# Two low-part subtractions per gate/up block handed from VectorE to accumulating transfers

## The chip, the cores and the metric

The kernel runs on one core of a Trainium2 chip. The metric is the device time of one execution in microseconds; the median of three runs of the kernel before is 1597.2 us (1596.22 to 1598.54).

## What is computed

One layer of a hybrid decoder block on 256 tokens of width 2048, in float32: an input projection, sliding-window attention beside a state-space mixer, two branch projections and a merged output projection, then the gated feed-forward part that the change touches, then a gated extra embedding and a last norm. The part that matters here:

```python
f = rmsnorm(h, g_ffn[i])
h = h + (jax.nn.silu(f @ w_gate[i]) * (f @ w_up[i])) @ w_down[i]
```

`w_gate` and `w_up` are 2048 x 5632, `w_down` is 5632 x 2048.

## The kernel before

Every float32 product is made of three matmuls in the fp32r type: weights and activations are each split into a high part (rounded to fp32r) and a low part (what rounding left), and high x high, high x low and low x high are summed in PSUM. So each weight chunk is loaded, cast to fp32r by ScalarE (the high part, tile `wh`), and subtracted by VectorE (the low part, tile `wl` = `wr` - `wh`).

Gate and up are computed by `wide_block` (L268), called by `hidden` (L987) once for each of the 11 column blocks of 512. A block takes the contraction dimension of 2048 in eight pairs of 128-row slices, `kp` = 0 to 7. For each pair there are two chunks, one of `w_gate` (`q` = 0) and one of `w_up` (`q` = 1), each 128 partitions x 1024 elements (512 KB).

- Pairs 0, 1, 3, 5 and 7 are plain: per chunk one load into `wr` (L293-294), the cast into `wh` (L296), the subtraction into `wl` (L298), and twelve matmuls of 512 columns (L248), so 24 matmuls per pair.
- Pairs 2, 4 and 6 use a seven-product scheme: VectorE first makes four sums of weight slices in `tr` (L316), then the two raw chunks and `tr` are split (L324, L325) into `wh`/`wl` and `th`/`tl`; 21 matmuls per pair.

So a block has 183 matmuls of 512 columns, and eight small transposes of the block before it run in its first pair.

Nothing in the source orders the engines against each other: the framework's scheduler sets the order of each engine's instructions, and the pools set how far ahead they may run. The pools that count here: `wraw` with 4 buffers (`wr`), `whi` with 4 (`wh`), `wlo` with 3 (`wl`), and `big` with 17 buffers of 8 KB per partition, which `tr`, `th`, `tl`, `mid` share with the activations that live through the stage. Weight loads are all issued by SP; in gate and up POOL has nothing to do.

The 11 blocks come in three thirds (4, 4 and 3 blocks); after each third, `nblock` (L178) multiplies its result with `w_down`.

Of the kernel before, what the change touches and what calls it, by code (L numbers as in the profile page):

```python
# [11 lines left out]
F32 = mybir.dt.float32  # L12
F32R = mybir.dt.float32r
I32 = mybir.dt.int32
AF = mybir.ActivationFunctionType
ALU = mybir.AluOpType
AX = mybir.AxisListType

P = 128
# [4 lines left out]
NB = 512  # L24
# [37 lines left out]
def block_kernel(ctx: ExitStack, tc: tile.TileContext, x, x_t, p_t, positions, vecs, rows, g_final,  # L62
                 w_in, w_attn_br, w_ssd_br, w_o, w_gate, w_up, w_down, w_ple_gate,
                 w_ple_proj, out):
    nc = tc.nc
# [3 lines left out]
    wraw_p = ctx.enter_context(tc.tile_pool(name="wraw", bufs=4))  # L69
    whi_p = ctx.enter_context(tc.tile_pool(name="whi", bufs=4))  # L70
    wlo_p = ctx.enter_context(tc.tile_pool(name="wlo", bufs=3))
# [5 lines left out]
    def big(shape, dtype=F32, name="big"):  # L77
        return big_p.tile(shape, dtype, name=name, tag="big")
# [186 lines left out]
        nc.vector.tensor_tensor(out=dst[:, :, 1], in0=fm, in1=dst[:, :, 0].bitcast(F32),  # L265
                                op=ALU.subtract)

    def wide_block(halves, lhs, nk, forms, pumps=1):  # L268

# [11 lines left out]
        def load(q, kp, dst):  # L283
            w, col0 = halves[q]
            nc.sync.dma_start(out=dst, in_=w[2 * kp * P:2 * (kp + 1) * P, col0:col0 + NB].rearrange(
                "(k p) n -> p k n", p=P))

        for kp in range(np_):
            ev, od = lhs(2 * kp), lhs(2 * kp + 1)
            tok = [[[x[:, t * P:(t + 1) * P] for x in k] for k in (ev, od)] for t in range(NT)]  # L290
            if kp not in forms:
                for q in range(2):
                    wr = wraw_p.tile([P, 2, NB], F32, name="wr", tag="wr")  # L293
                    load(q, kp, wr)
                    wh = whi_p.tile([P, 2, NB], F32R, name="wh", tag="wh")
                    nc.scalar.copy(out=wh, in_=wr)  # L296
                    wl = wlo_p.tile([P, 2, NB], F32R, name="wl", tag="wl")
                    nc.vector.tensor_tensor(out=wl, in0=wr, in1=wh.bitcast(F32), op=ALU.subtract)  # L298
                    for k in range(2):
                        for t in range(NT):  # L300
                            sums[2 * t + q].add(tok[t][k], (wh[:, k], wl[:, k]))
                    pump(pumps)
                continue
# [259 lines left out]
    for t in range(NT):  # L563
        nc.vector.scalar_tensor_tensor(out=dtv[:, t], in0=accs[1][t][:, W2 - SSM_H:W2],
                                       scalar=r1[:, t:t + 1],
                                       in1=row[:, R_DTB:R_DTB + SSM_H],
# [203 lines left out]
    for t in range(NT):  # L770
# [3 lines left out]
                             scale=r1[:, t:t + 1])  # L774
# [144 lines left out]
    for j in range(4):  # L919
        accs = nblock(w_in, GAO + j * NB, lhs_u, KD)  # L920
        for t in range(NT):
            nc.scalar.activation(out=merged[t][:, cols(j)], in_=accs[0][t], func=AF.Sigmoid,
                                 scale=r1[:, t:t + 1])
    drain(heads)
    r2 = const.tile([P, NT], F32, name="r2")
    for j in range(4):
        accs = nblock(w_attn_br, j * NB, lambda k: stat(attnT, k), 8)
        for t in range(NT):
            nc.vector.tensor_tensor(out=merged[t][:, cols(j)], in0=accs[0][t],
                                    in1=merged[t][:, cols(j)], op=ALU.mult)  # L930
# [14 lines left out]
    for j in range(4):  # L945
        accs = nblock(w_in, GSO + j * NB, lhs_u, KD)
        gs = [roll("gs") for _ in range(NT)]
        for t in range(NT):
            nc.scalar.activation(out=gs[t], in_=accs[0][t], func=AF.Sigmoid,
                                 scale=r1[:, t:t + 1])  # L950
# [35 lines left out]

    def hidden(j, dst):  # L987
        sums, parts = wide_block(((w_gate, j * NB), (w_up, j * NB)), lambda k: stat(hT, k), KD,
                                 hforms)
        act = [roll("act") for _ in range(NT)]  # L990
        for i, (o, op) in enumerate(((act[0], ALU.add), (parts[1], ALU.subtract),
                                     (act[1], ALU.add), (parts[3], ALU.subtract))):
            nc.vector.tensor_tensor(out=o, in0=sums[i], in1=parts[i], op=op)
        for t in range(NT):
            nc.scalar.activation(out=act[t], in_=act[t], func=AF.Silu, scale=r3[:, t:t + 1])
            nc.vector.scalar_tensor_tensor(out=act[t], in0=parts[2 * t + 1],
                                           scalar=r3[:, t:t + 1], in1=act[t], op0=ALU.mult,
                                           op1=ALU.mult)
        for i in range(2):
            side.append(lambda i=i: transpose_pair(act, i * 2 * P, dst, 2 * i))  # L1000
# [180 lines left out]
```

## Time and profile before

| | before |
|---|---|
| median of 3 runs | 1597.2 us (1596.22 to 1598.54) |
| the profiled execution's own time | 1597.2 us |
| its span in the trace | 1595.5 us |
| TensorE busy / VectorE busy / ScalarE busy | 99% / 69% / 51% |
| TensorE share of the chain that ended last | 95% |
| mean granted TensorE clock | 0.998 |
| bytes moved by DMA | 296.63 MB, mean 186 GB/s |

The busy share says who works all the time; the chain of waits says what the end of the kernel hung on. Matmuls are shown with their latency (0.39 us for 512 columns), and one starts before the last has ended, so that TensorE reads as busy even where it loses time between two starts. Lost time has to be looked for in the distance between starts, in the chain, and in the waits of the weight loads.

### The profile page before, as it was taken

The page shows a single profiled execution, that of the slowest core. Times are in us where ns is not written, and L with a number is a line of the kernel's source. Part 1 is how long each engine was busy: PE and PEld are TensorE (multiplying, and loading weights), DVE is VectorE, ACT ScalarE, POOL GpSimd, SP SyncE. Part 2 cuts the span into 40 slices and gives each one's busy share as a digit, 9 for nine tenths or more (in the row PEclk, how much of TensorE's full clock was granted, in tenths as well). Part 3 has the DMA queues.
Part 4 walks back from the last instruction along what each step waited for, and adds up shares of the span by engine and source line. Part 5 has one row for each costly group of instructions (what it writes and reads, how often), then busy time and mean ns, then how long its engine had stood idle before and what let it go on. Part 6 is the DMA issues. An engine that isn't in the chain of part 4 may idle for free.

```text
span 1595.5 us, 19878 instructions
## 1 busy us (share of the span) xinstructions
PE 1580.3 (99%) x7315; PEld 1304.8 (82%) x7315; DVE 1101.7 (69%) x1334; ACT 821.5 (51%) x1034; POOL 130.8 (8%) x136
## 2 busy tenths in 40 slices
PE   9999999999999999999999999999999999999997
PEld 7988888888888888888888888888888888887886
DVE  7776766666655555456788975598886578876673
ACT  6654665555643444445565553455554345546552
POOL 1014224143210000000000000000000000000000
PEclk9999999999999999999999999999999999999999
DMA  8666435555656666655566666666666666666661
GB/s 268 178 195 184 138 105 158 158 160 158 179 184 219 191 190 185 197 184 184 185 199 186 197 198 195 188 208 188 198 198 190 193 197 205 189 224 221 202 207 53
DMA packets 152564, 296.63 MB, mean 186 GB/s; under 512 B 9539, under 2 KB 9667, under 8 KB 152083
## 3 DMA queue, kind: packets, MB, share of 16 engines
q1 hardware_dynamic: 151168, 290.76, 58.9%
q0 software_dynamic: 576, 3.47, 0.7%
q8 instruction: 57, 0.93, 0.2%
q10 hardware_dynamic: 720, 1.14, 0.2%
q14 instruction: 43, 0.33, 0.1%
HBM read 293.23 MB, written 2.10 MB: 185 GB/s over the span
## 4 chain that ended last, share of the span: by engine, by line
PE 95%; DMA 1%; ACT 1%; DVE 1%; issue 1%; POOL 0%; POOLq 0%; DVEq 0%; ACTq 0%; SPq 0%
PE acc L204 17%; PE acc L206 17%; PE acc L205 17%; PE aux L248 15%; PE acc L248 14%; PE aux L205 2%; PE aux L204 2%; PE aux L206 2%; PE aux L150 1%; DMA wr<-in_w_down_dram 1%; PE aux L709 1%; DVE wl L195 1%; PE aux L886 1%; PE acc L233 1%; PE acc L234 0%
## 5 line engine op out<-in xcount | busy, mean ns | idle before, releaser
L195 DVE TENSOR_TENSOR wl<-wr,wh 128x1024 fp32r<-128x1024 f32 (+1 forms) x356 | 452.2, 1275 | 323.0 <-PE acc L205 251.8
L193 ACT CAST wh<-wr 128x1024 fp32r<-128x1024 f32 (+1 forms) x356 | 367.7, 1035 | 433.6 <-PE acc L206 343.4
L204 PE MATMUL acc<-wh,uT 128*128 128x512 f32 (+1 forms) x640 | 250.7, 392 | 0.6 <-ACT cb L438 0.6
L206 PE MATMUL acc<-wh,uT 128*128 128x512 f32 (+1 forms) x640 | 243.9, 381 | 0.0
L205 PE MATMUL acc<-wl,uT 128*128 128x512 f32 (+1 forms) x640 | 243.5, 381 | 0.0
L296 ACT CAST wh<-wr 128x1024 fp32r<-128x1024 f32 x110 | 115.7, 1053 | 144.9 <-PE acc L248 62.3
L248 PE MATMUL aux<-wh,hT 128*128 128x512 f32 x546 | 179.2, 391 | 0.0
L298 DVE TENSOR_TENSOR wl<-wr,wh 128x1024 fp32r<-128x1024 f32 x110 | 133.2, 1222 | 43.3 <-issue 33.8
L248 PE MATMUL acc<-wh,hT 128*128 128x512 f32 x466 | 155.0, 393 | 0.0
L204 PEld LDWEIGHTS acc<-wh,uT 128*128 128x128 f32 x640 | 120.3, 188 | 22.9 <-issue 1.4
L206 PEld LDWEIGHTS acc<-wh,uT 128*128 128x128 f32 x640 | 120.2, 188 | 23.0
L205 PEld LDWEIGHTS acc<-wl,uT 128*128 128x128 f32 x640 | 120.4, 188 | 22.4 <-issue 1.0
L248 PEld LDWEIGHTS aux<-wh,hT 128*128 128x128 f32 x546 | 102.3, 188 | 21.4
L248 PE MATMUL aux<-wl,hT 128*128 128x512 f32 x273 | 106.3, 390 | 0.0
L248 PEld LDWEIGHTS acc<-wh,hT 128*128 128x128 f32 x466 | 87.3, 188 | 18.1
L205 PE MATMUL acc<-wl,actT 128*128 128x512 f32 x256 | 99.8, 390 | 0.0
L206 PE MATMUL acc<-wh,actT 128*128 128x512 f32 x256 | 99.8, 390 | 0.0
L204 PE MATMUL acc<-wh,actT 128*128 128x512 f32 x256 | 99.6, 389 | 0.0
L248 PE MATMUL acc<-wl,hT 128*128 128x512 f32 x233 | 90.7, 389 | 0.0
L324 ACT CAST wh<-wr 128x1024 fp32r<-128x1024 f32 x66 | 55.2, 838 | 55.4 <-PE aux L248 18.1
L325 DVE TENSOR_TENSOR tl<-tr,th 128x2048 fp32r<-128x2048 f32 x33 | 75.5, 2288 | 6.4 <-ACT th L324 6.4
L324 ACT CAST th<-tr 128x2048 fp32r<-128x2048 f32 x33 | 63.0, 1910 | 14.9 <-DVE tr L316 13.0
(344 smaller groups left out, 2719.8 us busy)
## 6 DMA issues: line engine op xcount, KB each, us to landing
wr<-in_w_in_dram SPq DMA_DIRECT2D x144, 512.0 KB, 3.6
wr<-in_w_gate_dram SPq DMA_DIRECT2D x88, 512.0 KB, 3.8
wr<-in_w_up_dram SPq DMA_DIRECT2D x88, 512.0 KB, 4.4
wr<-in_w_down_dram SPq DMA_DIRECT2D x88, 512.0 KB, 4.5
wr<-in_w_ssd_br_dram SPq DMA_DIRECT2D x32, 512.0 KB, 3.9
wr<-in_w_o_dram SPq DMA_DIRECT2D x32, 512.0 KB, 4.4
wr<-in_w_ple_gate_dram SPq DMA_DIRECT2D x32, 512.0 KB, 4.4
wr<-in_w_in_dram SPq DMA_DIRECT2D x32, 256.0 KB, 4.1
```

What stands on the lines that cost most here:

```text
L150: nc.tensor.transpose(out=ps[:, j, t * P:(t + 1) * P], in_=src[t][:, c:c + P], identity=ident)
L193: nc.scalar.copy(out=wh, in_=wr)
L195: nc.vector.tensor_tensor(out=wl, in0=wr, in1=wh.bitcast(F32), op=ALU.subtract)
L204: nc.tensor.matmul(o, hi[:, ts], wh[:, kk, cs], start=(k == 0), stop=False)
L205: nc.tensor.matmul(o, hi[:, ts], wl[:, kk, cs], start=False, stop=False)
L206: nc.tensor.matmul(o, lo[:, ts], wh[:, kk, cs], start=False, stop=(k == nk - 1))
L233: nc.tensor.matmul(o, hi[:, ts], wh[:, i], start=(k == 0), stop=False)
L248: nc.tensor.matmul(self.tile, a, b, start=self.first, stop=self.left == 0)
L296: nc.scalar.copy(out=wh, in_=wr)
L298: nc.vector.tensor_tensor(out=wl, in0=wr, in1=wh.bitcast(F32), op=ALU.subtract)
L324: nc.scalar.copy(out=xh, in_=x)
L325: nc.vector.tensor_tensor(out=xl, in0=x, in1=xh.bitcast(F32), op=ALU.subtract)
```

## The change

In each block the low part of two plain `w_up` chunks, those of pairs 3 and 7, is no longer made by VectorE. `prepare` loads the chunk, ScalarE casts it into one half of a tile of the `big` pool (`both`), and writes the negative of the same rounded value into the other half (an activation with scale -1); then a DMA issued by POOL reads the chunk once more from HBM and adds it onto that half in SBUF. `early={0: 3, 4: 7}` says where it stands in the program: pair 3's chunk is prepared ahead of pair 0, pair 7's ahead of pair 4.

```diff
+        def prepare(q, kp):
+            w, col0 = halves[q]
+            wr = wraw_p.tile([P, 2, NB], F32, name="wr", tag="wr")
+            load(q, kp, wr)
+            both = big([P, 2, 2, NB], F32R, name="both")
+            wh, wl = both[:, 0], both[:, 1]
+            nc.scalar.copy(out=wh, in_=wr)
+            nc.scalar.activation(out=wl, in_=wr, func=AF.Copy, scale=-1.0)
+            nc.gpsimd.dma_start(out=wl, in_=w[2 * kp * P:2 * (kp + 1) * P, col0:col0 + NB].rearrange(
+                "(k p) n -> p k n", p=P), accum_op=ALU.add)
+            ready[q, kp] = wh, wl
+
+        ready = {}
         for kp in range(np_):
+            if kp in early:
+                prepare(1, early[kp])
...
                 for q in range(2):
-                    wr = wraw_p.tile([P, 2, NB], F32, name="wr", tag="wr")
-                    load(q, kp, wr)
-                    wh = whi_p.tile([P, 2, NB], F32R, name="wh", tag="wh")
-                    nc.scalar.copy(out=wh, in_=wr)
-                    wl = wlo_p.tile([P, 2, NB], F32R, name="wl", tag="wl")
-                    nc.vector.tensor_tensor(out=wl, in0=wr, in1=wh.bitcast(F32), op=ALU.subtract)
+                    if (q, kp) in ready:
+                        wh, wl = ready[q, kp]
+                    else:
...
-                                 hforms)
+                                 hforms, early={0: 3, 4: 7})
```

The scheduler orders the engines anew. Three places of the third block show it; the numbers behind the names are those of single tiles.

VectorE around pair 4, before. `wl_7157` and `wl_7175` are the low parts of pair 3 (gate, up), `wl_7199` and `wl_7201` those of pair 4's raw chunks, `wl_7235` and `wl_7253` those of pair 5, `tl_7203` the low part of pair 4's sums:

```order
L298 TENSOR_TENSOR wl_7157<-wr_7153,wh_7155 128x1024
L325 TENSOR_TENSOR tl_7125<-tr_7115,th_7124 128x2048
L298 TENSOR_TENSOR wl_7175<-wr_7171,wh_7173 128x1024
L316 TENSOR_TENSOR tr_7193<-wr_7189,wr_7190 128x512
L316 TENSOR_TENSOR tr_7193<-wr_7190 128x512
L325 TENSOR_TENSOR wl_7199<-wr_7189,wh_7198 128x1024
L316 TENSOR_TENSOR tr_7193<-tr_7193,wr_7189 128x512
L325 TENSOR_TENSOR wl_7201<-wr_7190,wh_7200 128x512
L316 TENSOR_TENSOR tr_7193<-tr_7193,wr_7189 128x512
L298 TENSOR_TENSOR wl_7235<-wr_7231,wh_7233 128x1024
L325 TENSOR_TENSOR tl_7203<-tr_7193,th_7202 128x2048
L298 TENSOR_TENSOR wl_7253<-wr_7249,wh_7251 128x1024
```

The same place with the change (`wl_7129` is the low part of pair 2's up chunk, `wl_7163` pair 3 gate, `wl_7205` and `wl_7207` pair 4, `wl_7241` pair 5 gate, `tl_7209` pair 4's sums):

```order
L346 TENSOR_TENSOR wl_7129<-wr_7118,wh_7128 128x512
L346 TENSOR_TENSOR tl_7131<-tr_7121,th_7130 128x2048
L318 TENSOR_TENSOR wl_7163<-wr_7159,wh_7161 128x1024
L337 TENSOR_TENSOR tr_7199<-wr_7195,wr_7196 128x512
L337 TENSOR_TENSOR tr_7199<-wr_7196 128x512
L346 TENSOR_TENSOR wl_7205<-wr_7195,wh_7204 128x1024
L337 TENSOR_TENSOR tr_7199<-tr_7199,wr_7195 128x512
L346 TENSOR_TENSOR wl_7207<-wr_7196,wh_7206 128x512
L337 TENSOR_TENSOR tr_7199<-tr_7199,wr_7195 128x512
L318 TENSOR_TENSOR wl_7241<-wr_7237,wh_7239 128x1024
L346 TENSOR_TENSOR tl_7209<-tr_7199,th_7208 128x2048
```

Pair 3's up chunk is gone from the list. With three `wlo` buffers a `wl` is written where the third `wl` before it stood: `wl_7235` takes the buffer of `wl_7175` (pair 3 up), `wl_7241` that of `wl_7163` (pair 3 gate).

TensorE at pair 4's products with the sums, before; `wh_7233` and `wl_7235` belong to pair 5:

```order
L248 MATMUL acc_7109<-th_7202,hforms_5620 128x512
L248 MATMUL acc_7110<-th_7202,hforms_5620 128x512
L248 MATMUL acc_7108<-th_7202,hforms_5620 128x512
L248 MATMUL aux_7019<-th_7202,hT_5618 128x512
L248 MATMUL aux_7017<-wh_7233,hT_5618 128x512
L248 MATMUL aux_7017<-wl_7235,hT_5618 128x512
L248 MATMUL acc_7109<-tl_7203,hforms_5620 128x512
L248 MATMUL acc_7109<-th_7202,hforms_5620 128x512
L248 MATMUL acc_7110<-tl_7203,hforms_5620 128x512
L248 MATMUL acc_7110<-th_7202,hforms_5620 128x512
```

and with the change:

```order
L248 MATMUL acc_7115<-th_7208,hforms_5620 128x512
L248 MATMUL acc_7115<-tl_7209,hforms_5620 128x512
L248 MATMUL acc_7115<-th_7208,hforms_5620 128x512
L248 MATMUL acc_7116<-th_7208,hforms_5620 128x512
L248 MATMUL acc_7116<-tl_7209,hforms_5620 128x512
L248 MATMUL acc_7116<-th_7208,hforms_5620 128x512
```

The count of matmuls is the same; the scheduler no longer moves products with `th` and two of pair 5 ahead of the first product with `tl`, which comes at the pair's eleventh matmul instead of its sixteenth.

ScalarE from pair 2's sums to pair 4's, before:

```order
L296 CAST wh_7155<-wr_7153 128x1024
L324 CAST th_7124<-tr_7115 128x2048
L296 CAST wh_7173<-wr_7171 128x1024
L324 CAST wh_7198<-wr_7189 128x1024
L324 CAST wh_7200<-wr_7190 128x512
L296 CAST wh_7233<-wr_7231 128x1024
L324 CAST th_7202<-tr_7193 128x2048
```

and with the change, where `both_7191` is pair 7's up chunk:

```order
L345 CAST th_7130<-tr_7121 128x2048
L316 CAST wh_7161<-wr_7159 128x1024
L296 CAST both_7191<-wr_7189 128x1024
L297 ACTIVATE both_7191<-wr_7189 128x1024
L345 CAST wh_7204<-wr_7195 128x1024
L345 CAST wh_7206<-wr_7196 128x512
L316 CAST wh_7239<-wr_7237 128x1024
L345 CAST th_7208<-tr_7199 128x2048
```

The accumulating DMA that POOL issues for `both_7191` waits for the second of its two rows. On SP the load of pair 7's up chunk takes the place in the queue that pair 3's had, and pair 3's stands ahead of pair 0's.

## Rows read from the trace of the kernel before

**Rows 1.** The page's busy times: engine, busy us, share of the span, instructions.

```profile
PE 1580.3 (99%) x7315; PEld 1304.8 (82%) x7315; DVE 1101.7 (69%) x1334; ACT 821.5 (51%) x1034; POOL 130.8 (8%) x136
```

**Rows 2.** The chain, two pairs of the third block: start us, us, what, count.

```profile
865.98 0.68 PE acc L248 x3
...
869.38 1.61 PE acc L248 x6
870.99 5.44 PE aux L248 x24
876.43 0.68 PE acc L248 x3
```

**Rows 3.** The chain, the same two pairs in the fifth block.

```profile
1039.37 0.68 PE acc L248 x3
...
1041.41 2.04 PE acc L248 x9
1043.45 6.12 PE aux L248 x27
1049.57 0.68 PE acc L248 x3
```

**Rows 4.** Waits from 700 to 1450 us: waiter <- releaser: us, times, longest.

```profile
PEld aux L248 <- DVE tl L325: 5.6, 15, 0.4
...
PEld acc L248 <- DVE tl L325: 4.2, 12, 0.4
```

**Rows 5.** Timeline of weight loads: start us, us, what [idle before <- releaser].

```profile
869.33 0.19 PEld L248 LDWEIGHTS acc<-tl,hforms 128*128 128x128 f32 x1 [0.37 <-DVE tl L325]
```

**Rows 6.** Timeline of VectorE in the third block.

```profile
859.38 1.28 DVE L316 TENSOR_TENSOR tr<-wr 128x512 f32<-128x512 f32 x2
...
864.17 0.69 DVE L325 TENSOR_TENSOR wl<-wr,wh 128x512 fp32r<-128x512 f32 x1
865.85 1.23 DVE L298 TENSOR_TENSOR wl<-wr,wh 128x1024 fp32r<-128x1024 f32 x1 [0.99 <-issue]
866.99 2.29 DVE L325 TENSOR_TENSOR tl<-tr,th 128x2048 fp32r<-128x2048 f32 x1
```

**Rows 7.** Timeline of ScalarE in the third block.

```profile
863.34 1.05 ACT L296 CAST wh<-wr 128x1024 fp32r<-128x1024 f32 x1 [2.15 <-PE aux L248]
864.30 1.90 ACT L324 CAST th<-tr 128x2048 fp32r<-128x2048 f32 x1
```

**Rows 8.** Timeline of TensorE around the first product with tl.

```profile
868.99 0.39 PE L248 MATMUL aux<-wl,hT 128*128 128x512 f32 x1
869.33 0.50 PE L248 MATMUL acc<-tl,hforms 128*128 128x512 f32 x1
869.67 0.39 PE L248 MATMUL acc<-th,hforms 128*128 128x512 f32 x1
```

**Rows 9.** Windows, one whole block: us, busy us (count) per engine, clock, DMA share, GB/s.

```profile
860.49:903.69 43.20, 43.20 (x192) 34.86 (x192) 38.36 (x44) 23.48 (x25) 0.00 (x0) 1.00 0.64 194
```

**Rows 10.** DMA issues: tile, queue, count, KB each, median us to landing.

```profile
wr<-in_w_up_dram SPq DMA_DIRECT2D x88, 512.0 KB, 4.4
...
gfin<-in_g_final_dram POOLq DMA_DIRECT2D x1, 1024.0 KB, 4.6
```

**Rows 11.** The page's DMA queues: packets, MB, share of 16 engines.

```profile
q1 hardware_dynamic: 151168, 290.76, 58.9%
```

**Rows 12.** The tile wr, 820 to 945 us: how long its loads took.

```profile
DMA to landing us min/median/max: 3.5/3.8/5.1
```

**Rows 13.** Timeline of POOL from 500 to 1460 us.

```profile
1335.77 0.59 POOL L1040 DMA_DIRECT2D pt<-in_p_t_dram  x1 [559.50 <-PE aux L150]
1398.29 0.53 POOL L1043 DMA_DIRECT2D gfin<-in_g_final_dram  x1 [61.93 <-DVE tl L325]
```

**Rows 14.** Timeline of ScalarE at the end of the first block's preparations.

```profile
774.94 0.61 ACT L264 CAST hforms<-fm 128x512 fp32r<-128x512 f32 x1
```

**Rows 15.** The chain in the first block: pair 2, and pair 4.

```profile
779.70 0.68 PE acc L248 x3
...
790.09 0.68 PE acc L248 x3
```

More of the change, by code (lines that the diff above doesn't have):

```diff
@@ L266, in token_forms, with wide_block @@
                                 op=ALU.subtract)
-    def wide_block(halves, lhs, nk, forms, pumps=1):
+    def wide_block(halves, lhs, nk, forms, pumps=1, early={}):
         psum.reverse()
@@ L292, in wide_block @@
                 for q in range(2):
-                    wr = wraw_p.tile([P, 2, NB], F32, name="wr", tag="wr")
-                    load(q, kp, wr)
-                    wh = whi_p.tile([P, 2, NB], F32R, name="wh", tag="wh")
-                    nc.scalar.copy(out=wh, in_=wr)
-                    wl = wlo_p.tile([P, 2, NB], F32R, name="wl", tag="wl")
-                    nc.vector.tensor_tensor(out=wl, in0=wr, in1=wh.bitcast(F32), op=ALU.subtract)
+                    if (q, kp) in ready:
+                        wh, wl = ready[q, kp]
+                    else:
+                        wr = wraw_p.tile([P, 2, NB], F32, name="wr", tag="wr")
+                        load(q, kp, wr)
+                        wh = whi_p.tile([P, 2, NB], F32R, name="wh", tag="wh")
+                        nc.scalar.copy(out=wh, in_=wr)
+                        wl = wlo_p.tile([P, 2, NB], F32R, name="wl", tag="wl")
+                        nc.vector.tensor_tensor(out=wl, in0=wr, in1=wh.bitcast(F32),
+                                                op=ALU.subtract)
                     for k in range(2):
```

## The prediction

> **What bounds the kernel now.** The page's busy times come first: TensorE is busy for 1580.3 of 1595.5 us, VectorE for 69% and ScalarE for 51% of the span [rows 1]. Removing VectorE work is therefore worth only what TensorE waits for it. A matmul's row lasts 0.39 us, but 24 of them take 5.44 us in the chain [rows 2, 8], so one starts every 0.227 us; time is lost where two starts stand further apart. In the chain I set two equal pieces of work side by side: pair 2 with pair 3 (21 + 24 matmuls) runs from 865.98 to 876.43 us in the third block, 10.45 us [rows 2], and from 1039.37 to 1049.57 us in the fifth, 10.20 us [rows 3], which is just 45 x 0.227. So 0.25 us is lost in the third block's pair.
>
> The timeline shows where. Between the matmul at 868.99 and the first with `tl` at 869.33 lie 0.34 us, and again 0.34 us to the next [rows 8]: twice 0.11 too much, as the weight load waited for `tl` [rows 5] and the load behind it could not be made ahead. `tl` takes VectorE 2.29 us and begins at 866.99, behind a `wl` of 1.23 us that itself began only at 865.85 after an idle 0.99 us [rows 6]. That `wl` is the next plain pair's gate chunk; it waited for a `wlo` buffer, the one of the last plain pair's up chunk, which TensorE finishes just before the seven-product pair starts. So the delay is not VectorE's load but its order: `tl` stands in line behind an instruction that waits for TensorE. The waits count 15 + 12 of these, 9.8 us of idle weight loads [rows 4]. By the order of the two engines 25 of the 33 seven-product pairs have this `wl` ahead of their `tl`; at 0.37 us each [rows 5] these are 9.25 of the 9.8 us, and two in the first block are smaller.
>
> **The change part by part.**
>
> *Removed: 22 subtractions of 1.22 us on VectorE* (1.23 in [rows 6]), two per block. A block has 38.36 us of VectorE work in 43.20 us [rows 9]; it becomes some 35.9. In itself this is worth nothing, as VectorE is not the bound.
>
> *Moved: what waits ahead of `tl`.* With the up chunk of pair 3 out of the `wlo` buffers, the `wl` ahead of pair 4's `tl` takes the buffer of pair 3's gate chunk, which is free twelve matmuls (2.7 us) earlier. Pair 7's up chunk does the same for the next block's start. By the order of the changed program only 2 `tl` still stand behind a `wl` that waits for the very end of the pair before: pair 6 of the first block and pair 2 of the second. In return TensorE wants `tl` five matmuls (1.1 us) earlier. That order is the one of the fifth block, where no time is lost [rows 3]. The term is 25 - 2 = 23 pairs x 0.25 = **5.75 us gained**; its ends are 0 (each wait replaced by another) and 27 x 0.25 = 6.75.
>
> *Is a new last wait close behind?* The tightest chain I find is pair 4's load. Its up chunk is loaded once VectorE has read pair 2's up chunk, whose `wl` waits for the gate half of pair 1. From the start of that half's last matmul but one: 0.4 us until it has ended, 0.69 for the `wl` [rows 6], 4.4 for the load [rows 10], then on VectorE four `tr` (1.28 + 2 x 0.69), a `wl` of 1.23 and one of 0.69, that is 4.6 [rows 6], `th` 1.90 on ScalarE [rows 7], `tl` 2.29: 14.3 us. TensorE reaches its first `tl` 69 matmuls later, at 69 x 0.227 = 15.6. **1.3 us to spare**: none at a load of 5.7 us. Loads of this stage took 3.5 to 5.1 us [rows 12], so it holds as long as the new transfers do not slow them.
>
> *Added on ScalarE: 22 activations*, priced like a cast of the same shape, 1.05 us [rows 7]. A block goes from 23.48 [rows 9] to 25.6 us of 43. They stand ahead of pair 4's casts, which TensorE needs some 45 matmuls (10 us) later. Nothing.
>
> *Added: 22 accumulating transfers of 512 KB.* No row shows such a transfer. By its bytes it is a plain load, 4.4 us; a plain 1 MB from POOL's queue landed in 4.6 us amid the weight loads [rows 10], so POOL's queue is no slower by itself. TensorE wants the tile late: in all blocks but the first the two casts stand at least 132 matmuls before the first product with it, 30 us, of which casts and issue take some 3, so that 27 us are left. In the first block the preparation stands behind the cast that ends at 775.55 [rows 14], so the transfer starts at about 778; pair 3's up half begins 12 matmuls ahead of pair 4, at about 787 [rows 15], 9 us. The wait itself costs nothing up to six times a plain load. POOL does nothing else here (idle 559.50 and 61.93 us ahead of two issues of under 0.6 [rows 13]), so none queues behind its waits but those two, used much later.
>
> *What it takes from the other loads* is the open price. The weight loads' 151168 packets took 58.9% of 16 engines [rows 11], so 0.1 us each; a chunk is 16 packets on each engine, 1.6 us. A block has 16 chunk loads for a DMA share of 0.64 [rows 9], 0.04 each. Two more at r times a plain packet's time make 0.64 + 0.08 r: 0.72 for r = 1, 0.80 for r = 2, full at r = 4.5. I take r = 2, as a sum has two operands to read where a copy has one, an assumption; the ends are 1 and 6.
>
> The Trainium skill (DMA: Bandwidth & Descriptors, "Issuing engines are not separate DMA queues") speaks against the change here: transfers of all issuing engines end up on the same 16 engines and interleave, so putting work on POOL's queue wins no bandwidth. The row of `gfin` can't contradict that, as it was one transfer; by the rule the price is the extra share above, and the sum stays as it is while r is small. The same page ("Anatomy of one DMA") would put a 512 KB transfer from POOL at 2.0 + 1.2 = 3.2 us, an estimate for a plain one; no run here shows an accumulating one.
>
> *SP* issues as many loads as before, each early chunk's in another's place. In the first block the chunk holds one of four `wr` buffers from 759 to 778 us, with plain pairs that need a load, a cast and a subtraction (some 6.7 us) per buffer: three buffers give a chunk every 2.2 us against 2.7 us of TensorE. Nothing.
>
> **Sum.** 1597.2 - 5.75 = **1591.5 us**. The profiled execution took 1597.2 us, 1.7 more than its span, and is the median itself.
>
> **The rivals.**
>
> *A. The accumulating transfers hold the DMA engines (slower).* Place: pair 5's gate load is released by the same ScalarE row that releases the transfer, and pair 4's `th` stands behind pair 5's cast in ScalarE's line. If half the transfer's 16 packets come between, the load is late by 8 x 0.1 x r. Some 2 us are free (1.3 above and a little ahead of `th`), so it decides from about r = 2.5 to 3 on. At r = 5, 4 us late, 2 us of stall per block in 10 blocks: +20, less 5.75, **about 1611 us**; at r = 4 about 1603. For it: no row gives r, and the share is already 0.64. Against it: r must be above 3. 0.22.
>
> *B. The gain is eaten (no change).* `tl` is on time, but margins of about 1 us at pairs 4 and 6 are used up in part by loads slower by a microsecond or two, or the waits of 0.25 come back at `wl` or `th`: half the gain at most, 1594.5 to 1599, **about 1596 us**. For it: the fifth block, with the same order, has a lighter beginning than the blocks inside a third. 0.18.
>
> *C. The forecast,* 0.60.
>
> That the change does not reach the engines is ruled out by the order above.
>
> **How the numbers follow.** A measurement of this kernel can tell about 0.2%, 3.2 us, from no change. The forecast and a small part of B's lower end are faster by more: 0.60. Same: 0.18. Slower: 0.22. The range goes from 1589.5 (all 27 waits and a little more) to 1605, which takes in B and the milder half of A; it leaves out some 0.15 above and 0.04 below. The forecast's own range is 1590 to 1593.5.
>
> **What would show it.** Right: the waits of weight loads for `tl` fall from 27 to a handful; pair 2 with pair 3 takes 10.20 us in every block; VectorE's busy time falls by 27 us, ScalarE's rises by 23; POOL's queue shows 22 issues that land within 27 us. Wrong in the first step: the waits for `tl` are gone and others of about 0.25 us stand in their place. Wrong in the price: the weight loads' median landing rises from 4.4 to over 6 us, the DMA share of a block nears 0.9, and `tl` waits for `th`, `th` for `wr`.

## The result and the profile after

The changed kernel takes **1617.1 us** in the median (1615.9 to 1618.4) against 1597.9 us of the kernel before on the same chip: the ratio is 1.012, with a 95% interval of 1.0103 to 1.0138. It is 19 us slower. The forecast was 1591.5 us, and the range ended at 1605.

The page of the kernel after, busy times (columns as in [rows 1]) and two DMA queues (packets, MB, share of 16 engines):

```profile
PE 1581.6 (98%) x7315; PEld 1306.0 (81%) x7315; DVE 1079.3 (67%) x1312; ACT 839.7 (52%) x1056; POOL 157.7 (10%) x158
...
q1 hardware_dynamic: 151168, 290.76, 56.7%
q0 software_dynamic: 6560, 15.00, 4.7%
```

The work moved the way that was foreseen, by a little less: VectorE lost 22.4 us (27 foreseen), ScalarE gained 18.2 (23 foreseen), POOL 26.9. The span grew by 21.2 us and TensorE's busy time by 1.3, so the time went into gaps between matmuls. The price of a packet is in the trace's packet records: the 5632 packets of 2 KB on POOL's queue, which are the new transfers', took 0.185 us on average, and the packets of 2 KB on SP's queue 0.102. An accumulating packet costs 1.8 plain ones; the prediction had taken 2.

The DMA issues of the kernel after (tile, queue, count, KB each, median us to landing):

```profile
wr<-in_w_up_dram SPq DMA_DIRECT2D x88, 512.0 KB, 4.8
wr<-in_w_gate_dram SPq DMA_DIRECT2D x88, 512.0 KB, 4.9
...
both<-in_w_up_dram POOLq DMA_DIRECT2D x22, 512.0 KB, 8.9
```

and the gate chunks' line of the kernel before:

```profile
wr<-in_w_gate_dram SPq DMA_DIRECT2D x88, 512.0 KB, 3.8
```

The new transfers land after 8.9 us, twice a plain load, and the other loads' medians rose less: from 4.4 [rows 10] to 4.8 for the up chunks, from 3.8 to 4.9 for the gate chunks. Who waits shows in the waits from 765 to 1450 us (waiter <- releaser: us, times, longest):

```profile
PEld aux L248 <- DVE wl L346: 10.8, 7, 2.5
...
PEld acc L248 <- DVE wl L346: 7.2, 4, 2.2
...
PEld aux L248 <- DMA both<-in_w_up_dram: 3.1, 1, 3.1
PEld acc L248 <- DVE tl L346: 2.9, 5, 0.9
...
PEld aux L248 <- DVE tl L346: 0.4, 1, 0.4
```

The 27 waits for `tl` [rows 4] are down to six. In their place stand eleven for a `wl` of line 346, up to 2.5 us long, nine of them at pair 6 of a block, and one for the tile `both` in the first block. Of the 21.3 us by which the 11 blocks grew (table below), 15.2 stand ahead of such a `wl` in ten places, and the first block has 5.0. The timeline of the kernel after at pair 6 of the seventh block, all engines:

```profile
1140.37 1.20 POOL L298 DMA_DIRECT2D both<-in_w_up_dram  x1 [19.92 <-ACT both L297]
...
1144.39 0.37 SPq L286 DMA_DIRECT2D wr<-in_w_gate_dram  x1
1145.00 0.37 SPq L286 DMA_DIRECT2D wr<-in_w_up_dram  x1
...
1150.43 1.05 ACT L345 CAST wh<-wr 128x1024 fp32r<-128x1024 f32 x1 [2.19 <-DMA wr<-in_w_gate_dram]
1151.77 1.30 DVE L337 TENSOR_TENSOR tr<-wr 128x512 f32<-128x512 f32 x2 [2.16 <-DMA wr<-in_w_up_dram]
...
1158.52 2.29 DVE L346 TENSOR_TENSOR tl<-tr,th 128x2048 fp32r<-128x2048 f32 x1 [1.98 <-ACT th L345]
1159.21 0.39 PE L248 MATMUL aux<-wh,hforms 128*128 128x512 f32 x1
1160.73 0.68 DVE L346 TENSOR_TENSOR wl<-wr,wh 128x512 fp32r<-128x512 f32 x1
...
1161.47 0.50 PE L248 MATMUL aux<-wl,hforms 128*128 128x512 f32 x1 [1.86 <-DVE wl L346]
```

Read from the bottom. TensorE should go on at 1159.44 and goes on at 1161.47, 2.03 us late: it wants the `wl` of pair 6's up chunk, a row of 0.68 us that stands behind the 2.29 us of `tl`. `tl` waits for `th`, `th` for `tr`, and `tr` had waited 2.16 us for the load of the up chunk. That load and the gate chunk's, issued at 1145.00 and 1144.39, are used 6.8 and 6.0 us later. What they met is in the trace's packet records, counted by the microsecond in which they start (the first column is the start of that microsecond, on the clock of the views):

```
us     POOL's queue: packets, mean us   SP's queue: packets, mean us
1143      0                                184, 0.091
1144      5, 0.190                         151, 0.093
1145     92, 0.188                          19, 0.053
1146    102, 0.178                           0
1147     68, 0.144                          81, 0.087
1148      5, 0.147                         207, 0.079
1149      0                                201, 0.083
1150      0                                214, 0.079
1151      0                                106, 0.075
```

The transfer issued at 1140.37 begins to move its data 4.5 us later, just as SP issues pair 6's loads, and from 1145.30 to 1147.40 us no plain packet starts. Then three loads (pair 7's gate chunk was issued at 1146.76) run together until 1152. The other blocks are alike: from the second block on pair 6's two loads took 4.9 to 7.0 us, in the kernel before 3.6 to 4.8. The window from 1139 to 1150 us says the same (columns as in [rows 9]; the last three are granted clock, DMA share and GB/s); first the kernel after, then before:

```profile
1139.00:1150.00 11.00, 11.00 (x50) 8.96 (x49) 9.43 (x10) 6.34 (x7) 1.20 (x1) 1.00 0.90 258
```

```profile
1139.00:1150.00 11.00, 11.00 (x48) 8.84 (x49) 9.36 (x10) 6.12 (x7) 0.00 (x0) 1.00 0.66 210
```

The Trainium skill (DMA: Bandwidth & Descriptors, "Queues, rings and completion order") says that an engine switches between queues only after a whole packet of some 9 to 17 descriptors. A transfer has 256 of these records, 16 for each of 16 engines; if a record is a descriptor, by that rule one transfer would be served in about one go. The trace doesn't settle it: the two empty microseconds above agree, but of the ten transfers of pair 7's chunks behind the first block only four have a stretch of about 2 us in which no plain packet starts, the others of 0.2 to 1.1 us, and no record here shows the switch itself.

A second loss followed one of the stalls. In the last block two starts stand 2.4 us apart; then the granted clock is near its lower level, 1.2 GHz, for 3 us, and matmuls start every 0.427 us in place of 0.227, about 1.5 us lost. That window of the kernel after:

```profile
1427.50:1430.50 3.00, 3.00 (x9) 2.35 (x8) 3.00 (x4) 0.18 (x1) 0.00 (x0) 0.54 0.71 232
```

And the first block, TensorE's timeline of the kernel after at the first product with the early chunk:

```profile
784.15 0.39 PE L248 MATMUL aux<-both,hT 128*128 128x512 f32 x1
787.21 0.96 PE L248 MATMUL aux<-both,hT 128*128 128x512 f32 x3 [2.67 <-DMA both<-in_w_up_dram]
```

Here two starts stand 3.1 us apart, and the granted clock stayed at 1.00 (787.2 to 790.6 us).

### The profile page after: what moved, and what is told of

Same layout as the page of the kernel before. It is cut to its first block, busy times and chain, and to the rows that moved or that the text cites. A ratio compares the mean times of both kernels' runs of the same rounds, so it can differ in the third digit from the quotient of the medians.

```text
span 1616.7 us, 19916 instructions
## 1 busy us (share of the span) xinstructions
PE 1581.6 (98%) x7315; PEld 1306.0 (81%) x7315; DVE 1079.3 (67%) x1312; ACT 839.7 (52%) x1056; POOL 157.7 (10%) x158
## 5 line engine op out<-in xcount | busy, mean ns | idle before, releaser
L248 PE MATMUL aux<-wh,hT 128*128 128x512 f32 x450 | 149.9, 391 | 0.0
L205 PEld LDWEIGHTS acc<-wl,uT 128*128 128x128 f32 x640 | 120.4, 188 | 22.4 <-issue 1.0
L316 ACT CAST wh<-wr 128x1024 fp32r<-128x1024 f32 x88 | 92.4, 1050 | 84.0 <-DMA wr<-in_w_gate_dram 32.3
L248 PE MATMUL acc<-wh,hT 128*128 128x512 f32 x386 | 130.2, 392 | 0.0
L318 DVE TENSOR_TENSOR wl<-wr,wh 128x1024 fp32r<-128x1024 f32 x88 | 106.8, 1221 | 19.8 <-ACT wh L316 8.2
L248 PEld LDWEIGHTS aux<-wh,hT 128*128 128x128 f32 x450 | 84.5, 188 | 17.5
L248 PE MATMUL aux<-wl,hT 128*128 128x512 f32 x225 | 87.7, 390 | 0.0
L345 ACT CAST wh<-wr 128x1024 fp32r<-128x1024 f32 x66 | 54.3, 833 | 60.5 <-DMA wr<-in_w_gate_dram 19.1
L298 POOL DMA_DIRECT2D both<-in_w_up_dram x22 | 26.5, 1204 | 603.4 <-ACT both L297 409.8
L248 PEld LDWEIGHTS acc<-wh,hT 128*128 128x128 f32 x386 | 72.5, 188 | 14.9
```

The costliest lines, as they stand in the source:

```text
L205: nc.tensor.matmul(o, hi[:, ts], wl[:, kk, cs], start=False, stop=False)
L248: nc.tensor.matmul(self.tile, a, b, start=self.first, stop=self.left == 0)
L298: nc.gpsimd.dma_start(out=wl, in_=w[2 * kp * P:2 * (kp + 1) * P, col0:col0 + NB].rearrange("(k p) n -> p k n", p=P), accum_op=ALU.add)
L345: nc.scalar.copy(out=xh, in_=x)
```

## The experiments

**Theory 1**: the accumulating packets run just when pair 6's loads want the engines; with VectorE's new order (`wl` behind `tl`) the whole delay reaches TensorE. Rivals: the new order or the two ScalarE rows alone; any accumulating transfer, wherever it stands.

To compare runs, this table gives for each of the 11 blocks the time from the start of its first to that of its last of 183 matmuls, from one profiled execution each. The shortest seen are 42.2 us, and 41.25 in blocks 5 and 9, which have no transposes inside.

| block | 1 | 2 | 3 | 4 | 5 | 6 | 7 | 8 | 9 | 10 | 11 | sum |
|---|---|---|---|---|---|---|---|---|---|---|---|---|
| before | 42.70 | 43.01 | 42.97 | 42.97 | 41.25 | 43.06 | 42.98 | 42.97 | 41.25 | 43.06 | 42.98 | 469.2 |
| changed | 47.68 | 43.46 | 43.57 | 44.06 | 44.97 | 44.03 | 44.71 | 44.28 | 42.80 | 44.57 | 46.33 | 490.5 |
| no transfer (e1) | 42.96 | 42.49 | 42.21 | 42.21 | 41.27 | 42.46 | 42.37 | 42.21 | 42.25 | 43.12 | 42.21 | 465.8 |
| only pair 3 (e7) | 45.19 | 42.54 | 42.52 | 42.53 | 41.31 | 42.91 | 42.53 | 42.52 | 41.25 | 43.61 | 42.44 | 469.4 |
| moved by some 5 us (e13) | 46.83 | 42.79 | 42.21 | 42.37 | 45.17 | 42.62 | 42.21 | 42.23 | 45.05 | 42.28 | 42.21 | 476.0 |

**e1: no transfer.** The changed kernel without its DMA; the low part of 22 chunks stays minus the high part, so the chunk itself is left out of it. Every engine's order but POOL's is that of the changed kernel.

```diff
-            nc.gpsimd.dma_start(out=wl, in_=w[2 * kp * P:2 * (kp + 1) * P, col0:col0 + NB].rearrange(
-                "(k p) n -> p k n", p=P), accum_op=ALU.add)
```

> The accumulating transfers are left out, so the low part of these 22 chunks stays minus the high part; the casts, the early loads and the order of every engine are those of the change. Theory 'engines' (the transfers' packets delay the loads of pair 6, whose chain then stops TensorE): the stalls at pair 6 and in the first block go, loads land in about 4.4 us, and the time falls below that of the kernel before, to about 1592 us. Theory 'order' (the new order puts the low part of pair 6's up chunk behind tl, and that chain is too long by itself): the stall of 1 to 2 us at pair 6 stays, about 1612 us. Theory 'ScalarE' (the 22 more activations delay the casts): stays slow too, since they are all still there.

Measured: 1596.5 us (ratio to before 0.9991, 0.9982 to 1.0001). The whole loss is gone with the transfer, so the order and the ScalarE rows together cost next to nothing by themselves; but the time is 4.5 us above what theory 'engines' expected, so most of the forecast gain is missing as well. The longest waits for `tl` and `wl` in this run; the one for `wl` stands at pair 6 of the ninth block, and no other for a `wl` is over 0.3 us:

```profile
PEld acc L248 <- DVE tl L344: 1.3, 3, 0.8
PEld aux L248 <- DVE wl L344: 1.1, 1, 1.1
```

This run is also the ceiling of the idea in this order: with a transfer that costs nothing the kernel gains 1.6 us, not 5.75.

**e2: a plain transfer.** The same DMA without the addition (the low part is then the chunk itself): same bytes, same queue, same orders.

```diff
-                "(k p) n -> p k n", p=P), accum_op=ALU.add)
+                "(k p) n -> p k n", p=P))
```

> The same transfers with the same bytes, queue and place, but without the addition (the low part becomes the rounded chunk itself). Theory 'engines': a packet takes some 0.10 us in place of 0.18, so about half of the delay is left: 1600 to 1608 us, landing of the transfer about 7 us. If the addition alone were to blame: about 1592 us. Theory 'order': as slow as the change, about 1617 us.

Measured: 1598.1 us (1.0002, 0.9993 to 1.0011), below the 1600 to 1608 that theory 'engines' expected. Its median landing:

```profile
both<-in_w_up_dram POOLq DMA_DIRECT2D x22, 512.0 KB, 6.7
```

Twenty-two plain chunks more on the engines cost 1.6 us together (against e1), though from the second block on pair 6's loads are issued as long behind the transfers as in the changed kernel, 3.9 to 6.6 us; here they took 3.6 to 5.9. What harms is the addition: 2.2 us more to landing, and packets of nearly twice the time.

**e3: the up chunk's `wl` ahead of `tl`.** In the seven-product pairs of the changed kernel, `tl` is kept behind that `wl` on VectorE.

```diff
-                nc.vector.tensor_tensor(out=xl, in0=x, in1=xh.bitcast(F32), op=ALU.subtract)
+                with tc.issue_after(low.ins) if x is tr else ExitStack():
+                    low = nc.vector.tensor_tensor(out=xl, in0=x, in1=xh.bitcast(F32),
+                                                  op=ALU.subtract)
```

> The change with one issue edge: in pairs 2, 4 and 6 tl stands behind the low part of the up chunk. Theory 'engines' alone: pair 6's chain still begins with late loads, and now tl is the last: it ends some 0.7 us later than in the change but is needed three matmuls later, so the stall goes from about 1.6 to about 1 us, 1610 us. Theory 'order' alone: the stalls at pair 6 go, about 1600 us with those of the first block left.

Measured: 1606.4 us (1.0056, 1.0038 to 1.0074), 10.7 less than the changed kernel and between the two expectations. The stalls at pair 6 now stand at `tl` and are shorter:

```profile
PEld acc L248 <- DVE tl L347: 5.7, 10, 1.3
...
PEld aux L248 <- DVE tl L347: 5.1, 6, 1.2
```

So about half of the loss needs the new order. It is an amplifier: without the transfer (e1) the same order has one such wait of 1.1 us in all blocks.

**e4: the kernel before with `tl` in front.** The next pair's gate `wl` is kept behind `tl`, with no early chunk and no transfer: the gain that the prediction saw, had by order alone.

```diff
-                    nc.vector.tensor_tensor(out=wl, in0=wr, in1=wh.bitcast(F32), op=ALU.subtract)
+                    with tc.issue_after(tl_op.ins) if tl_op and q == 0 else ExitStack():
+                        nc.vector.tensor_tensor(out=wl, in0=wr, in1=wh.bitcast(F32),
+                                                op=ALU.subtract)
```

> The kernel before with one issue edge and no transfer: the low part of the next pair's gate chunk stands behind tl, so that no wait for a wlo buffer stands ahead of tl. If the 25 waits of 0.25 us are those of this order, they go and the time falls by about 6 us, to about 1592 us. If another last wait is close behind: no change, 1596 to 1599 us.

Measured: 1623.4 us (1.015, 1.0133 to 1.0167), far from both expectations. The `wl` that waits frees its raw buffer later, and the load behind it starts later; ScalarE's casts then wait for gate loads, which is no row of note in the kernel before:

```profile
ACT wh L296 <- DMA wr<-in_w_gate_dram: 81.1, 22, 5.6
```

This way of removing a wait of 0.25 us for `tl` costs more than the wait; other orders were not tried. The stage lives on loads that are released just in time.

**e5 to e8: where the transfers stand.** e5 prepares pair 7's chunk one pair later, e6 does that and leaves the first block without early chunks, e7 has only pair 3's chunk, e8 only pair 7's.

```diff
-                                 hforms, early={0: 3, 4: 7})
+                                 hforms, early={0: 3, 5: 7})
```

That is e5; in e6 the table is `{0: 3, 5: 7} if j else {}`, in e7 `{0: 3}`, in e8 `{4: 7}`.

> The change with pair 7's chunk prepared ahead of pair 5 instead of ahead of pair 4: the two ScalarE rows and the transfer stand behind pair 4's th, some 4 us later, and VectorE has pair 6's wl of the up chunk ahead of tl in every block. Theory 1 (collision: pair 7's transfer moves its data while pair 6's loads are on the way, and pair 6's wl stands behind tl): pair 6's stalls go, about 15 us; the first block's loss of some 6 us stays: 1600 us, 1597 to 1604. Rival 1 (every accumulating transfer costs TensorE its share wherever it stands, (1617.1 - 1596.5)/22 = 0.94 us each): 22 of them still cost 20.6 us, 1615 to 1619.

Measured: 1611.2 us (1.0067, 1.0042 to 1.0091), above what theory 1 expected. The stalls at pair 6 are gone (the one wait for such a `wl` that is left stands at pair 2 of the fifth block); others came. The two rows for `both` now stand behind pair 4's `th` in ScalarE's line, the loads around them are late again, and the blocks' first transposes wait for `act`. ScalarE's and TensorE's timeline of e5 at the end of the third block:

```profile
894.40 1.05 ACT L316 CAST wh<-wr 128x1024 fp32r<-128x1024 f32 x1 [3.23 <-DMA wr<-in_w_gate_dram]
...
904.88 0.33 PE L150 MATMUL aux<-ident,act 128*128 128x128 f32 x1 [0.85 <-DVE act L1017]
```

> As the run with pair 7 prepared ahead of pair 5, and with no early chunk in the first block (20 transfers). Theory 1: the first block has no wait for a tile, no second load of its chunks: another 5 to 6 us less, 1594 to 1598 us. Rival 1 (0.94 us for every transfer): 1596.5 + 20 x 0.94 = 1615 us.

Measured: 1606.1 us (1.0044, 1.0029 to 1.006). The first block's early chunks cost about 5 us (1611.2 to 1606.1; 4.1 in that block's own time), as expected; but the time is 8 us above the 1594 to 1598 of theory 1, which is what e5 missed too.

> The change with pair 3's chunk alone (11 transfers, prepared ahead of pair 0); pair 7's up chunk is subtracted by VectorE again. Theory 1: the transfers lie over the block's start and not over pair 6's loads, and wl stands ahead of tl at pair 6 in all blocks but two: 1597 plus the first block's 5 us, 1599 to 1604, and no stall of over 1 us at pair 6. Rival 1: 1596.5 + 11 x 0.94 = 1607 us, spread over the blocks.

Measured: 1598.9 us (1.0003, 0.9994 to 1.0013), against the rival's 1607. Eleven accumulating transfers at the blocks' starts cost 2.5 us in the first block (table) and next to nothing later.

> The change with pair 7's chunk alone (11 transfers, prepared ahead of pair 4); pair 3's up chunk is subtracted by VectorE again, and pair 6's wl stands ahead of tl. Theory 1: the loads of pair 6 still come late under the transfer, but only tl hangs on it, about 0.5 to 1 us in each of ten blocks as in the run with the order changed: 1601 to 1607 us, the loss at pair 6. Rival 1: 1607 us, but spread. Rival 2 (the order alone made the loss, the transfer none): 1596 to 1598 us.

Measured: 1601.4 us (1.0016, 1.0004 to 1.0029). With `wl` ahead of `tl` the eleven transfers at pair 6's place still cost about 3 us, at `tl`: 31 waits of weight loads for it, 15.3 us, against 27 and 9.8 in the kernel before [rows 4]. A price for each transfer as such is excluded: 11 cost 0.7 in one place, 3 in another, and 19 for both sets in the changed order.

**e9: half the addition.** Only the first of the chunk's two slices is added, 256 KB.

```diff
-            nc.gpsimd.dma_start(out=wl, in_=w[2 * kp * P:2 * (kp + 1) * P, col0:col0 + NB].rearrange(
-                "(k p) n -> p k n", p=P), accum_op=ALU.add)
+            nc.gpsimd.dma_start(out=wl[:, 0], in_=w[2 * kp * P:(2 * kp + 1) * P, col0:col0 + NB],
+                                accum_op=ALU.add)
```

> The changed kernel with the accumulating transfer cut to the first of the chunk's two slices (256 KB, 8 packets on each DMA engine instead of 16); the second slice's low part stays minus the high part, so half of the sum is left out of 22 chunks. No engine's order changes. Theory 1 (what counts is how long the 16 DMA engines serve nothing but the accumulating packets, 16 x 0.18 = 2.9 us in the changed kernel): now 1.45 us, less than the plain transfer's 1.6 that cost nothing; pair 6's loads come some 1.5 us sooner and most of the stall is gone: 1599 to 1605 us, landing of the transfer about 6.5 us. Rival (the delay sits in the addition as such, at issue or on the tile, and not in the engines' time): the landing stays near 8.9 us and the time above 1610 us.

Measured: 1602.3 us (1.0031, 1.0017 to 1.0045), landing 6.8 us. Half the packets leave 28% of the loss ((1602.3 - 1596.5) / (1617.1 - 1596.5)). So the rival, a landing near 8.9 us and a time above 1610, is out, and the loss grows faster than the time for which the accumulating packets take the engines. But that time is not the whole measure, as theory 1 had it: here it is 8 x 0.18 = 1.5 us for a transfer and the loss against e1 is 5.8 us; in e2 it is 16 x 0.10 = 1.6 us and the loss 1.6. What makes the difference is open.

**e10: pair 3's chunk, but not in the first block.**

```diff
-                                 hforms, early={0: 3, 4: 7})
+                                 hforms, early={0: 3} if j else {})
```

> The run with pair 3's chunk alone, and no early chunk in the first block (10 transfers, VectorE does the rest). Theory 1 (pair 3's transfers collide with nothing, the first block's wait for the tile is its only loss): 1598.9 less 2.5 us, 1595 to 1597.5 us, level with the kernel before or a hair below it. Rival (the transfers of pair 3 also cost a little in each block and the wait in the first block hides other delays): 1598 to 1600 us.

Measured: 1596.7 us (0.9988, 0.9978 to 0.9997). It is the fastest version found that computes the whole result, 1.6 us under the kernel before and within 0.2% of it.

**e11 and e12: the transfer later, two misses.** POOL is given work ahead of pair 7's transfer; the other engines keep their order.

```diff
-            nc.scalar.activation(out=wl, in_=wr, func=AF.Copy, scale=-1.0)
+            nc.scalar.activation(out=wl, in_=wr, func=AF.Copy,
+                                 scale=-0.25 if kp == 7 else -1.0)
+            if kp == 7:
+                for _ in range(2):
+                    nc.gpsimd.tensor_tensor(out=wl, in0=wl.bitcast(F32), in1=wl.bitcast(F32),
+                                            op=ALU.add)
```

> The changed kernel with two POOL additions of 128 x 1024 (about 2.8 us each) ahead of the transfer of pair 7's chunk (its low half is started at a quarter, each addition doubles it). All other engines keep their order; the transfer starts some 5.6 us later, and its data move after pair 6's loads instead of ahead of them. Theory 1 (collision in time): pair 6's loads take their usual 4 to 4.5 us, the ten stalls at pair 6 go, 15 us less, of which a few come back where the next loads now meet the transfer: 1601 to 1608 us. Rival (the order with wl behind tl, or the two ScalarE rows, make the stall whatever the transfer does): pair 6 stalls as before, 1615 to 1619 us.

Measured: 1645.5 us (1.0302, 1.0276 to 1.0328), worse than either theory. The additions held VectorE up, and TensorE waited 2.1 us for `tl` at pair 4 in ten blocks. The timeline of e11, POOL and VectorE side by side:

```profile
1151.35 4.56 POOL L301 TENSOR_TENSOR both<-both 128x1024 fp32r<-128x1024 f32 x2 [19.13 <-ACT both L297]
1151.78 4.68 DVE L342 TENSOR_TENSOR tr<-wr 128x512 f32<-128x512 f32 x2
```

The two `tr` rows take 4.68 us instead of 1.28 [rows 6], until POOL is done. The Trainium skill (SBUF — State Buffer, "Who interferes with whom") says that a VectorE instruction with two SBUF inputs contends with a GpSimd instruction that reads SBUF; this row agrees. The run says nothing on the theories.

e12 has small work instead:

```diff
+            if kp == 7:
+                for _ in range(40):
+                    nc.gpsimd.tensor_tensor(out=wl[:, 0, :2], in0=wl[:, 0, :2].bitcast(F32), in1=ones,
+                                            op=ALU.mult)
```

> The changed kernel with forty POOL multiplications by one on two columns of the tile, ahead of the transfer of pair 7's chunk: at 0.1 to 0.2 us each the transfer starts 4 to 8 us later, and POOL touches next to nothing, so VectorE is not held up as in the run with two large additions. All other engines keep their order. Theory 1 (collision in time): the accumulating packets run after pair 6's loads instead of ahead of them, those loads take 4 to 5 us, the stalls at pair 6 go: 15 us less, some of which comes back at the next loads: 1601 to 1609 us. Rival (the order with wl behind tl and the two ScalarE rows make the stall whenever the packets run): 1615 to 1619 us.

Measured: 1690.2 us (1.0574, 1.0557 to 1.0592). One multiplication on two columns took about 0.6 us, not 0.1 to 0.2 (a row on two tiles of that size, `r` of line 176, takes POOL 0.8 us in the changed kernel already), so the forty took some 24 us, the transfer came that much later, and TensorE waited for the tile. The timeline of e12, POOL and TensorE, and then the window behind the wait:

```profile
1129.80 22.07 POOL L300 TENSOR_TENSOR both<-both,ones 128x2 fp32r<-128x2 f32 x37
...
1159.80 1.62 PE L248 MATMUL acc<-both,hT 128*128 128x512 f32 x3 [5.53 <-DMA both<-in_w_up_dram]
```

```profile
1160.00:1164.00 4.00, 4.00 (x10) 3.13 (x11) 0.41 (x1) 0.00 (x0) 0.00 (x0) 0.50 0.88 219
```

The size was wrong, but one thing can be read: with the order unchanged, the gaps ahead of the `wl` of an up chunk in a seven-product pair fell from 15.2 us (ten) to 3.3 (four), counted as what two starts of matmuls stand apart beyond 0.227 us. The two longest of the four, 1.28 us each, stand at pair 2 of blocks 5 and 9, behind transfers of pair 3's chunk, which had not been delayed; at pair 6 alone the gaps fell from 13.5 us to 0.8. These gaps belong to the moment of the transfer.

**e13 and e14: the transfer some 5 us later.** Eight multiplications instead of forty; e14 has no early chunk in the first block.

```diff
-                for _ in range(40):
+                for _ in range(8):
```

> As the run with forty small multiplications on POOL, with eight: at the 0.53 us each that one took there, the transfer of pair 7's chunk starts 4.2 us later than in the changed kernel and lands some 8 us before it is wanted. Theory 1 (collision in time): pair 6's loads are served ahead of the accumulating packets; the 15 us of stalls at pair 6 fall to 3 or 4 as with forty, nothing waits for the tile after the first block, and a few us come back where pair 7's loads meet the packets: 1600 to 1607 us. Rival (any place of the packets inside the block costs as much): 1614 to 1619 us.

Measured: 1604.7 us (1.004, 1.0025 to 1.0055), in the middle of what theory 1 expected and 10 us from the rival. The timeline of e13 at the seventh block's pair 6, SP and POOL:

```profile
1136.56 0.37 SPq L286 DMA_DIRECT2D wr<-in_w_gate_dram  x1
1137.16 0.37 SPq L286 DMA_DIRECT2D wr<-in_w_up_dram  x1
1137.76 1.20 POOL L302 DMA_DIRECT2D both<-in_w_up_dram  x1 [0.30 <-POOL both L300]
```

The loads are now issued 0.6 and 1.2 us ahead of the transfer, where they were 4 us and more behind it, and TensorE has no stall there. Blocks 3, 7, 8 and 11 take 42.2 us, the floor (table). What is left are blocks 5 and 9 with two such stalls each, at pairs 2 and 6, 7.7 us longer together than before, and the first block. In blocks 5 and 9 the transfer was still issued 1.6 us ahead of the first of pair 6's loads, which took 5.5 to 5.9 us; in the other blocks behind the first they took 3.7 to 5.5.

> The same, with no early chunk in the first block (20 transfers). Theory 1: the run before less the first block's 5 us, 1596 to 1602 us, level with the kernel before at best, as the run without any transfer gave 1596.5. Rival (any place of the packets costs as much): 1610 to 1615 us.

Measured: 1602.5 us (1.0022, 1.0012 to 1.0032), a little above what was expected: blocks 5 and 9 were 1.1 and 1.5 us longer than in e13 and took back part of the first block's gain.

## Why the prediction was wrong, step by step

**What bounds the kernel** was read rightly: VectorE's load is not the bound (22 us of it removed and 1.6 gained, e1), and `tl` stood behind a `wl` that waits for TensorE.

**The term of 5.75 us** had the right mechanism and was too large. In e1 the waits for `tl` are all but gone, and blocks 3, 4, 8 and 11 each gain 0.76 us, three pairs by 0.25 as predicted. But blocks 2, 6 and 7 gain 0.5 to 0.6, and blocks 1, 9 and 10 lose 0.26, 1.00 and 0.06: another last wait stood there. The stage gains 3.4 us, and the median 1.6. The table is one execution each: before's is 0.9 us under its median and e1's 1.9, which is 1.0 of the other 1.8; where the remaining 0.8 went is not settled.

**The step that failed is "Is a new last wait close behind?"** It looked at pair 4 alone, found 1.3 us to spare up to a load of 5.7 us, and took the loads of this stage, 3.5 to 5.1 us [rows 12], as what the change would meet. The chain that counts is pair 6's. There the new order puts the `wl` of the up chunk behind `tl`, which the prediction had not looked up in the order; no time is left (of 2.16 us that the load was late, 2.03 reached TensorE), and the loads took 6.0 and 6.8 us. The 5.1 came from a window of 125 us; over all blocks the longest gate or up load took 5.5 us before and 9.4 after.

**The price of the transfers** had the right packet (1.8 for the assumed 2; the reason given for 2 was not tested) and the wrong measure. The mean DMA share of a block even stayed below the 0.80 computed: 0.70 from 1120 to 1163 us after. But a transfer's packets come together, 4 us after its issue, and a mean over 43 us does not show whom they hit: over 11 us the share was 0.90. The signs that the prediction named for a wrong price, a median landing of over 6 us and a share near 0.9 for a block, did not come (4.8 and 4.9 us, 0.70), only the chain did, `tl` behind `th` behind `tr` behind `wr`. Nor was POOL's queue "no slower by itself", as the prediction read from one transfer: the plain 512 KB of e2 landed after 6.7 us, against its 4.4 and the 3.2 of its other estimate.

**Rival A** (0.22) was right in kind: the transfers hold the engines and delay a load that is released at the same time. Its place and point were wrong. It named pair 5's gate load and a packet price of 2.5 to 3 as the point from which it decides, with 1603 us at 4 and 1611 at 5; the loads hit were pair 6's, and 1.8 was enough for 1617.

**The first block's 9 us of cover** was too little. The transfer was issued at 778.11 us and took 9.1, so the tile came at 787.2; with the new order TensorE wanted it at 784.4, not at 787. Measured against e1 the block is 4.7 us longer: 2.8 is this wait, and 1.5 a wait for `th` at pair 4, whose loads took 7.6 and 8.2 us behind the first transfer.

**The two ScalarE rows** cost nothing that e1 can tell where the change has them; e5, where they stand behind pair 4's `th`, is slower, and how much of that is theirs is not shown.

## What to carry to other kernels

A transfer that is late itself can be harmless and still cost 1%: ask not when it lands but which loads are released while its packets run, and how much slack the tightest of these has. A mean DMA share says nothing on that; take a window as long as one load. Where a stage's loads are released just in time, work taken from an engine that is not the bound gains only the few tenths by which it was last in line, and e1-like runs (the new cost removed, the order kept) give that ceiling first.

## What the runs showed of the hardware

- An accumulating transfer of 512 KB from HBM onto SBUF lands after 8.9 us amid these loads; a plain one from POOL's queue after 6.7 us (e2), SP's loads after 3.8 and 4.4 in the kernel before. Its packet of 2 KB takes 0.185 us against 0.10, and POOL is busy for 1.20 us with the issue, against 0.71 for the plain one (e2).
- The data of the accumulating transfers began to move 2.5 to 4.9 us after their issue, those of the plain ones of e2 2.4 to 4.1 us after it.
- Two VectorE additions of 128 x 512 took 4.68 us instead of 1.28 while POOL added in place on SBUF (e11).
- A POOL multiplication on 128 x 2 elements took about 0.6 us in the row above (22.07 us for 37 of them), 0.53 in the mean of all 440 in e12; eight of them took 2.3 us in the first block of e13 and 5.0 in most others.
- The granted clock was at its lower level (0.54 and 0.50 in the windows above, 1.2 GHz) for 3 to 5 us after two starts of matmuls had stood 2.4 us (this kernel's last block), 2.8 (e13's first block, 0.50 from 787.2 to 790.5 us) and 5.9 us apart (e12). After 2.7 us in e7's first block and 3.1 in this kernel's it stayed at 1.00. So these runs give no length of a gap from which it falls.
